# Three input tiles on ScalarE's queue, memory sums and recurrence constant on GpSimd, memory norm spread behind the first value block

## The chip, the cores and the metric

The kernel runs on one core of a Trainium2 chip. The time is that of the device, in microseconds (us), for one execution. The engines are named as the profile names them: PE is TensorE (matrix products), PEld its weight loads, DVE is VectorE, ACT is ScalarE, POOL is GpSimd, SP is SyncE, which only issues DMAs here. Each engine takes its own instructions in a fixed order and waits for the others through semaphores.

## The reference

A two-layer decoder trunk over 1024 positions of width 1024, all in float32. Layer A joins a gated linear recurrence (width 768) with an attention of four heads over 256 memory rows; layer B joins a windowed attention with the same kind of memory attention. Each has an output projection and a SwiGLU feed-forward behind it. What the change touches is the start of layer A:

```python
mem_n = rms_norm(mem, mem_norm)
h = x
for l in range(DEPTH):
    hn = rms_norm(h, norm_mix_pre[l])
    mkv = mem_n @ w_mem_kv[l]
    mk = mkv[..., :MEM_WIDTH].reshape(bsz, n_mem, MEM_HEADS, HEAD_DIM)
    mv = mkv[..., MEM_WIDTH:].reshape(bsz, n_mem, MEM_HEADS, HEAD_DIM)
    if l < N_A_LAYERS:
        proj = hn @ w_in_a[a]
        ...
        y = rg_lru(xr, w_r, b_r, w_i, b_i, lam) * jax.nn.gelu(gate)
    ...
    m_out = memory_attention(mq, mk, mv)
```

In `rg_lru` the decay is `exp(8 * r * log_sigmoid(lam))`. Its `8 * log_sigmoid(lam)` and twice that are the recurrence constant, 6 columns of 128 numbers.

## The kernel before

Activations lie with their 1024 channels on partitions, in 8 tiles of 128, and positions along the row, in two halves of 512. Every matrix product in float32 is made of three: a number is split into a rounded high part (a cast or scaled copy on ScalarE) and a low part (the difference, on VectorE), and TensorE adds low x high, high x high and high x low. So each weight and each activation costs a ScalarE and a VectorE instruction before TensorE can use it. In a tile's name `ah`/`al` are the activation's parts, `wh`/`wl` a weight's, `wraw` the weight as loaded. The names `qs`, `pb`, `ph` are buffers that hold weight parts in the opening (`spare`).

The order on each engine comes from a scheduler that simulates a timeline and is steered by priorities, by `after` (this instruction not before that one) and by `pin`/`place`, which set an instruction among the matmuls collected in `self.mms` at given places.

The opening (`layer_a`, L1033 on) runs like this:

- `inputs(0, ...)` loads the eight tiles of `x` for the first half, one DMA each (L1043, all on SyncE's queue), between pieces of the first two weights (L141). ScalarE makes `ah` (L1048), VectorE `al` (L1049). Then come eight squares on ScalarE (L234, L237), summed on VectorE (L238).
- `rstd` ends a norm: ones-matmuls put the sums into a column (L248), VectorE scales it (L252), GpSimd takes the power -1/2 (L253), and `spread` multiplies it out over 128 partitions on TensorE (L260), from where ScalarE copies it (L264). `rcn` is the first norm's column, `rcm` the memory's. `self.marks` collects these matmuls so that they can be placed.
- `mem_queries` (L447) makes the two memory queries, in the buffers `gt`, with the tiles as they arrive. `lru_in` makes the two products of the first recurrence block (`mm`, L163 to L165).
- `lambda_const` computes the constant by a series, 28 instructions on VectorE of 6 columns each, which may start behind the first norm's column (`prev`, the mean).
- `mem_in` loads the memory in four DMAs (L1061), splits it (L1066, L1067), squares it on ScalarE (L220, L223) and sums it on VectorE (L224).
- `mem_kv` makes the memory's keys (two blocks, L345 to L347, scaled by the spread norm on VectorE, L348) and values (two blocks, L355 to L357, scaled by the column `rcm` on ScalarE, L358). `mem_expand` casts the keys to both halves of the partitions (`mkh`, L321) and takes the low parts (`mkl`, L323).
- The second recurrence block's two products follow, each 24 matmuls, with weights cast at L94 and L95.

Four rules of the code matter. A buffer is given again only when its last reader is done: `gt` has two, `mm` three, `wh` and `wl` two, `wraw` two. The table load on ScalarE stands ahead of the first activation. The instructions of `mem_in` stand behind the first tiles' squares by `after`. And GpSimd had, from the constants at the start to 60 us, only the two powers and the copies of three columns between halves (`halo`, L464).

Of the kernel before, what the change touches and what calls it, by code (L numbers as in the profile page):

```python
# [10 lines left out]
ALU = mybir.AluOpType  # L11
AX = mybir.AxisListType

P = 128
D = 1024
T = 1024
H = 512
KT = D // P
NM = 256
# [24 lines left out]
POST_STEPS = range(4, 20, 2)  # L44
LATE_PRODUCTS, LAST_STEPS = (2, 5, 3), range(36, 132, 12)
OUT_PARTS = {1: (0, 0), 2: (1, 0), 3: (1, 0), 4: (1, 1), 5: (1, 1), 6: (0, 0), 7: (0, 1)}
NO_SYNC = mybir.DependencyInfo(mybir.DependencyClass.NoSync, mybir.DependencyReason.DATA)
SHUF = list(range(8, 16)) + list(range(0, 8)) + list(range(16, 32))


class Trunk:
# [232 lines left out]
        self.mhalf = cp.tile([P, 4], F32, name="mhalf")  # L284
        nc.gpsimd.memset(self.mhalf, -0.5)

    def lambda_const(self, prev):
        nc, cp = self.nc, self.cp
        lam = self.cst[:, C_LAM:C_LAM + NL]
        t = [self.t(f"lam{i}", (P, NL)) for i in range(5)]  # L290
        e, d, s, s2, h = t
        nc.scalar.activation(e, lam, AF.Abs)
        self.table(e, e, AF.Exp, scale=-1.0)
        self.after(nc.vector.tensor_scalar(d, e, 2.0, None, op0=ALU.add), prev)
        nc.vector.reciprocal(d, d)
        nc.vector.tensor_tensor(s, e, d, op=ALU.mult)
        nc.vector.tensor_tensor(s2, s, s, op=ALU.mult)
        self.after(nc.vector.memset(h, 1.0 / 19.0), prev)
# [3 lines left out]
        nc.vector.tensor_tensor(h, h, s, op=ALU.mult)  # L302
        self.after(nc.vector.tensor_scalar(d, lam, 0.0, None, op0=ALU.min), prev)
# [3 lines left out]
        nc.vector.tensor_scalar(self.cl2, self.cl, 16.0, None, op0=ALU.mult)  # L307
        nc.vector.tensor_scalar(self.cl, self.cl, 8.0, None, op0=ALU.mult)

    def kdup_far(self, kf, r, kh, kl, prev):  # L310
        here = slice(r, r + 64)
# [15 lines left out]
        nc.scalar.copy(qs[r:r + 64], qf[r:r + 64])  # L327
        nc.vector.tensor_tensor(qs[64 - r:128 - r], qf[r:r + 64], qs[r:r + 64].bitcast(F32), op=ALU.subtract)

    def mem_kv(self, layer, mact, rcm, rsm):  # L330
        nc = self.nc
        kf, vf = (self.t(t).rearrange("p (i c) -> p i c", i=2) for t in ("gr", "gi"))
        for j in range(2):
            if layer == 0:
                with self.tc.high_priority(offset=WEIGHT_LEAD):
                    w, piece = self.first_weight(self.a["wmk"][layer, j], self.spare(1 - j))
                    for i in range(2):
                        piece(4 * i, 4 * i + 4)
            else:
                whole = self.weight(self.a["wmk"][layer, j])  # L340
                w = [[x[:, 4 * i:4 * i + 4] for x in whole] for i in range(2)]
            ps = self.psum("mm")
            for k in range(KT):
                wh, wl = (x[:, k % 4] for x in w[k // 4])
                nc.tensor.matmul(ps[:, :NM], wh, mact[k][1], start=k == 0, stop=False)  # L345
                nc.tensor.matmul(ps[:, :NM], wh, mact[k][0], start=False, stop=False)
                nc.tensor.matmul(ps[:, :NM], wl, mact[k][0], start=False, stop=k == KT - 1)  # L347
            nc.vector.tensor_tensor(kf[:, j], ps[:, :NM], rsm, op=ALU.mult)  # L348
        wv = [self.weight(self.a["wmv"][layer, :, 4 * j:4 * j + 4], k=4) for j in range(2)]
        for m in range(2):  # L350
            ps = self.psum("mm")
            for k in range(KT):
                wh, wl = wv[k // 4]
                ms = slice(m * P, m * P + P)
                nc.tensor.matmul(ps[:, :NM], mact[k][1][:, ms], wh[:, k % 4], start=k == 0, stop=False)  # L355
                nc.tensor.matmul(ps[:, :NM], mact[k][0][:, ms], wh[:, k % 4], start=False, stop=False)
# [673 lines left out]
    def layer_a(self):  # L1030
        nc, a = self.nc, self.a
# [4 lines left out]
        def inputs(n, before=()):  # L1036
            act, xs, loads = [], [], []
            s = self.t("s")
            for k in range(KT):
                if k in before:  # L1040
                    before[k]()
                x = self.acc_tile()
                loads.append(nc.sync.dma_start(x, a["xT"][k * P:k * P + P, n * H:n * H + H]))  # L1043
# [4 lines left out]
                last = nc.scalar.activation(ah, x, AF.Copy, scale=g)  # L1048
                nc.vector.scalar_tensor_tensor(al, x, g, ah.bitcast(F32), op0=ALU.mult, op1=ALU.subtract)  # L1049
            take = self.sums([(nc.vector, s)], "00000000", ("sq", "sp"))  # L1050
            for k in range(KT):
                ins = take(k, xs[k]) if k == 0 else (take(k, xs[k]), self.square)[1]
                self.after(ins, last)
            return act, self.rstd(s, f"n{n}", "rsn")[1], loads

        def mem_in(square, summed):
            act = []
            s = self.t("s")[:, :NM]
            for q in range(4):
# [21 lines left out]
        mean, prev = self.mean, (self.square, self.summed)  # L1081
        marks = self.marks[:2]
        self.mms = []
        for n in range(2):
# [9 lines left out]
            for j0 in range(0, NL, 2):  # L1094
                cur = []
                for j in (j0, j0 + 1):
# [275 lines left out]
```

## Time and profile before

| | |
|---|---|
| three runs | 1968.11, 1966.99, 1969.09 us; median 1968.11 us |
| the profiled execution | 1966.76 us, its span (first to last instruction) 1964.7 us |
| granted TensorE clock | 0.997 |
| DMA | 361.71 MB, 184 GB/s over the span |
| VectorE, GpSimd busy | 71%, 22% of the span |

Rows of the timeline have the start, the duration, engine, line of the kernel, operation, output and inputs with their shapes, and in brackets how long the engine was idle before and what ended that. A stretch has its length, the busy time of PE, PEld, DVE, ACT and POOL with their counts, the granted clock, the DMA engines' busy share and GB/s. Busy time of TensorE overlaps from one matmul to the next: a matmul of 512 columns lasts 0.39 us and the next one starts 0.23 us behind it.

### The profile page before, as it was taken

Reading aid. Unit: us, or ns where it says so; the run is one execution under the profiler, and the core shown is the slowest. Engines: PE = TensorE matmul, PEld = TensorE weight load, DVE = VectorE, ACT = ScalarE, POOL = GpSimd, SP = SyncE. Lnnn points to the kernel's source line nnn. Section 1 sums busy time; section 2 is a strip of 40 time slices with the busy share of each in tenths; the row PEclk is TensorE's granted clock in tenths of the full one; section 3 lists DMA queues with packets and bytes.
Section 4 is the critical chain, followed back from the end, with each engine's and each line's share of the span. In section 5 each row is a group of like instructions: output and inputs, shape, how many; then the busy total and the mean of one; then the engine's idle time right before and its main releaser. Section 6 shows DMA issues by size and latency. Waiting matters only on the chain.

```text
span 1964.7 us, 27857 instructions
## 1 busy us (share of the span) xinstructions
PE 1935.3 (99%) x9382; PEld 1626.5 (83%) x9382; DVE 1397.8 (71%) x2319; ACT 1015.5 (52%) x1939; POOL 426.0 (22%) x435
## 2 busy tenths in 40 slices
PE   8999999999999999999999999999999999999997
PEld 7887888788888888888788888887888888888887
DVE  8888977976776676455786898669656666754566
ACT  6677974534444444454554778554333333344551
POOL 0122100034443330000035454100223232300001
PEclk9999999999999999999999999999999999999999
DMA  5522536167767789775563333361644544586653
GB/s 186 170 86 81 158 121 228 67 233 250 240 243 276 257 294 319 236 230 176 201 214 141 121 106 108 107 258 43 209 135 166 167 150 157 199 302 195 218 187 129
DMA packets 184686, 361.71 MB, mean 184 GB/s; under 512 B 20448, under 2 KB 26336, under 8 KB 184544
## 3 DMA queue, kind: packets, MB, share of 16 engines
q1 hardware_dynamic: 184544, 359.95, 53.8%
q8 instruction: 73, 1.20, 0.2%
q14 instruction: 69, 0.57, 0.1%
HBM read 251.86 MB, written 105.91 MB: 182 GB/s over the span
## 4 chain that ended last, share of the span: by engine, by line
PE 88%; DVE 6%; ACT 2%; issue 2%; DMA 1%; POOL 1%; SPq 0%; POOLq 0%; DVEq 0%; ACTq 0%
PE mm L699 12%; PE mm L701 12%; PE mm L700 12%; PE mm L807 7%; PE mm L808 7%; PE mm L809 7%; PE mm L165 6%; PE mm L163 6%; PE mm L164 6%; PE oo L1187 1%; PE tt L1180 1%; PE oo L248 1%; PE mm L679 1%; PE mm L678 1%; PE mm L680 1%
## 5 line engine op out<-in xcount | busy, mean ns | idle before, releaser
L94 ACT CAST ch<-wq 128x512 fp32r<-128x512 f32 x311 | 193.4, 622 | 423.6 <-PE mm L700 212.4
L95 DVE TENSOR_TENSOR cl<-wq,ch 128x512 fp32r<-128x512 f32 x311 | 236.2, 760 | 191.8 <-ACT ch L94 118.3
L699 PE MATMUL mm<-al,ch 128*128 128x512 f32 x640 | 249.6, 390 | 2.9 <-ACT c L729 2.9
L700 PE MATMUL mm<-ah,ch 128*128 128x512 f32 x640 | 249.2, 389 | 0.0
L701 PE MATMUL mm<-ah,cl 128*128 128x512 f32 x640 | 249.0, 389 | 0.0
L163 PE MATMUL mm<-al,wh 128*128 128x512 f32 x552 | 218.2, 395 | 0.6 <-ACT wh L94 0.6
L165 PE MATMUL mm<-ah,wl 128*128 128x512 f32 x552 | 216.9, 393 | 0.9 <-DVE wl L95 0.9
L164 PE MATMUL mm<-ah,wh 128*128 128x512 f32 x552 | 216.8, 393 | 0.0
L807 PE MATMUL mm<-tl,ch 128*128 128x512 f32 x532 | 207.4, 390 | 0.6 <-ACT ah L909 0.3
L808 PE MATMUL mm<-th,ch 128*128 128x512 f32 x532 | 207.0, 389 | 0.0
L809 PE MATMUL mm<-th,cl 128*128 128x512 f32 x532 | 206.4, 389 | 0.0
L699 PE MATMUL mm<-tl,ch 128*128 128x512 f32 x480 | 187.4, 390 | 0.2
L701 PE MATMUL mm<-th,cl 128*128 128x512 f32 x480 | 186.5, 389 | 0.4 <-DVE cl L95 0.4
L700 PE MATMUL mm<-th,ch 128*128 128x512 f32 x480 | 186.8, 389 | 0.0
L710 DVE TENSOR_TENSOR c<-c,mm 128x512 f32<-128x512 f32 x120 | 82.3, 686 | 100.7 <-PE mm L701 100.5
L699 PEld LDWEIGHTS mm<-al,ch 128*128 128x128 f32 x640 | 120.2, 188 | 28.4 <-ACT c L729 3.7
L701 PEld LDWEIGHTS mm<-ah,cl 128*128 128x128 f32 x640 | 120.2, 188 | 25.0
L700 PEld LDWEIGHTS mm<-ah,ch 128*128 128x128 f32 x640 | 120.2, 188 | 24.7
L165 PEld LDWEIGHTS mm<-ah,wl 128*128 128x128 f32 x552 | 103.7, 188 | 23.4 <-DVE wl L95 2.1
L719 POOL TENSOR_TENSOR x<-wq,wq 128x512 f32<-128x512 f32 x36 | 52.6, 1461 | 318.7 <-DMA wq<-in_wi_dram 310.8
L163 PEld LDWEIGHTS mm<-al,wh 128*128 128x128 f32 x552 | 103.8, 188 | 21.1 <-ACT wh L94 1.0
L164 PEld LDWEIGHTS mm<-ah,wh 128*128 128x128 f32 x552 | 103.8, 188 | 20.2
(415 smaller groups left out, 4312.4 us busy)
## 6 DMA issues: line engine op xcount, KB each, us to landing
wq<-in_wi_dram SPq DMA_DIRECT2D x168, 256.0 KB, 4.6
xz<-hd SPq DMA_DIRECT2D x154, 256.0 KB, 4.1
th<-xz SPq DMA_DIRECT2D x154, 256.0 KB, 3.5
wp<-in_wf_dram SPq DMA_DIRECT2D x112, 256.0 KB, 4.1
wz<-wp SPq DMA_DIRECT2D x88, 256.0 KB, 2.3
wq<-wz SPq DMA_DIRECT2D x56, 256.0 KB, 3.5
wraw<-in_wa_dram SPq DMA_DIRECT2D x26, 512.0 KB, 3.5
wq<-in_wf_dram SPq DMA_DIRECT2D x42, 256.0 KB, 4.0
```

Source lines behind the costliest of these rows:

```text
L94: self.cast = self.nc.scalar.copy(hi, src)
L95: return (eng or self.nc.vector).tensor_tensor(lo, src, hi.bitcast(F32), op=ALU.subtract)
L163: self.mms += [nc.tensor.matmul(out, wh, al, start=i == 0, stop=False), nc.tensor.matmul(out, wh, ah, start=False, stop=False), nc.tensor. ...
L164: nc.tensor.matmul(out, wh, ah, start=False, stop=False),
L165: nc.tensor.matmul(out, wl, ah, start=False, stop=i == len(ks) - 1)]
L699: ins += [mm(out, wh, xl, start=start and k == 0, stop=False, skip_group_check=not start), mm(out, wh, xh, start=False, stop=False, skip_g ...
L700: mm(out, wh, xh, start=False, stop=False, skip_group_check=not start),
L701: mm(out, wl, xh, start=False, stop=k == 3, skip_group_check=not start)]
L710: add = lambda o, x, y: nc.vector.tensor_tensor(o, x, y, op=ALU.add)
L807: ins += [mm(ps[m], wh[:, m], xl[:, cs], start=start and p == 0, stop=False, skip_group_check=not start), mm(ps[m], wh[:, m], xh[:, cs], s ...
L808: mm(ps[m], wh[:, m], xh[:, cs], start=False, stop=False, skip_group_check=not start),
L809: mm(ps[m], wl[:, m], xh[:, cs], start=False, stop=p == NFB // 2 - 1, skip_group_check=not start)]
```

## The change

Four edits. The first three input tiles of the first half are issued on ScalarE's queue (`HEAD`). `lambda_const` runs on GpSimd but for the reciprocal and the two activations, without its order behind the mean; the fused multiply-add of its end becomes two instructions. The memory's sums run on GpSimd. In the first layer's `mem_kv` the two key blocks are accumulated in `gt` buffers, and the memory norm's spread is ordered behind the last matmul of the first value block.

```diff
+HEAD = 3
...
-    def lambda_const(self, prev):
-        nc, cp = self.nc, self.cp
+    def lambda_const(self):
+        nc, cp, po = self.nc, self.cp, self.nc.gpsimd
...
         self.table(e, e, AF.Exp, scale=-1.0)
-        self.after(nc.vector.tensor_scalar(d, e, 2.0, None, op0=ALU.add), prev)
+        po.tensor_scalar(d, e, 2.0, 0.0, op0=ALU.add, op1=ALU.add)
         nc.vector.reciprocal(d, d)
-        nc.vector.tensor_tensor(s, e, d, op=ALU.mult)
-        nc.vector.tensor_tensor(s2, s, s, op=ALU.mult)
-        self.after(nc.vector.memset(h, 1.0 / 19.0), prev)
+        po.tensor_tensor(s, e, d, op=ALU.mult)
+        po.tensor_tensor(s2, s, s, op=ALU.mult)
+        po.memset(h, 1.0 / 19.0)
         for q in (17, 15, 13, 11, 9, 7, 5, 3, 1):
-            nc.vector.tensor_tensor(h, h, s2, op=ALU.mult)
-            nc.vector.tensor_scalar(h, h, 1.0 / q, None, op0=ALU.add)
...
+            po.tensor_tensor(h, h, s2, op=ALU.mult)
+            po.tensor_scalar(h, h, 1.0 / q, 0.0, op0=ALU.add, op1=ALU.add)
...
-        nc.vector.scalar_tensor_tensor(self.cl, h, -2.0, d, op0=ALU.mult, op1=ALU.add)
...
+        po.tensor_scalar(h, h, -2.0, 0.0, op0=ALU.mult, op1=ALU.add)
+        po.tensor_tensor(self.cl, h, d, op=ALU.add)
...
-    def mem_kv(self, layer, mact, rcm, rsm):
+    def mem_kv(self, layer, mact, rcm, rsm, spread=None):
...
-            ps = self.psum("mm")
+            ps = self.psum("mm" if spread is None else "gt")
...
-                nc.tensor.matmul(ps[:, :NM], mact[k][0][:, ms], wl[:, k % 4], start=False, stop=k == KT - 1)
+                last = nc.tensor.matmul(ps[:, :NM], mact[k][0][:, ms], wl[:, k % 4], start=False, stop=k == KT - 1)
+            if m == 0 and spread is not None:
+                self.after(spread[0], last)
...
-                loads.append(nc.sync.dma_start(x, a["xT"][k * P:k * P + P, n * H:n * H + H]))
+                queue = nc.scalar if n == 0 and k < HEAD else nc.sync
+                loads.append(queue.dma_start(x, a["xT"][k * P:k * P + P, n * H:n * H + H]))
...
-                    self.sumsq(s, mr[:, i], k == 0, NM, ("sp", "sq")[i])
+                    self.sumsq(s, mr[:, i], k == 0, NM, ("sp", "sq")[i], nc.gpsimd)
...
-                        self.lambda_const(mean)
+                        self.lambda_const()
                         mem = mem_in(*prev)
-                        kvf = self.mem_kv(0, *mem)
+                        kvf = self.mem_kv(0, *mem, self.marks[-1])
```

How the order on the engines moves, at three places. First ScalarE at its start; `acc` are the input tiles, `lam` the constant. Before:

```order
L292 ACT_TABLE_LOAD
L292 ACTIVATE lam_65_370<-cst 128x6
L98 ACTIVATE lam_65_370<-lam_65_370 128x6
L94 CAST wh_131<-wraw_130 128x256
L1048 ACTIVATE ah_144<-acc_142,cst 128x512
```

And with the change:

```order
L1048 DMA acc_142<-in_xT_dram 128x512
L1048 DMA acc_154<-in_xT_dram 128x512
L1048 DMA acc_163<-in_xT_dram 128x512
L1053 ACT_TABLE_LOAD
L1053 ACTIVATE ah_144<-acc_142,cst 128x512
L293 ACTIVATE lam_65_370<-cst 128x6
L95 CAST wh_131<-wraw_130 128x256
L1053 ACTIVATE ah_156<-acc_154,cst 128x512
```

Three DMA issues and the table load now stand ahead of the first tile's scaled copy, and the constant's first activation behind it. The table load carries that copy's wait for `cst`.

Second GpSimd around the first norm's power (`rcn`). Before:

```order
L459 MEMSET xr_1021 128x3
L253 TENSOR_TENSOR rcn_45_232<-rcn_45_232,mhalf 128x4
L464 COPY halo_116<-xr_308 128x3
L253 TENSOR_TENSOR rcm_465<-rcm_465,mhalf 128x2
L459 MEMSET xr_1242 128x3
```

With the change, from the end of the constant on:

```order
L308 TENSOR_TENSOR cl<-lam_69_374,lam_66_371 128x6
L309 TENSOR_SCALAR cl_403<-cl 128x6
L310 TENSOR_SCALAR cl<-cl 128x6
L225 TENSOR_TENSOR s_408<-s_408,sq_418 128x256
L254 TENSOR_TENSOR rcn_45_232<-rcn_45_232,mhalf 128x4
L225 TENSOR_TENSOR s_408<-s_408,sp_427 128x256
L225 TENSOR_TENSOR s_408<-s_408,sq_432 128x256
```

The whole constant and the first of the seven memory sums now stand ahead of that power; the other six sums stand between it and the memory's power. On TensorE the spread of `rcn` (L261) now follows the twelfth matmul of the second product at once, and all the memory's key matmuls follow that product; before, fourteen of them stood between.

Third ScalarE and TensorE behind the memory norm's spread. ScalarE before (`gi` is the first value block, `xc` the spread, `gr` the keys):

```order
L358 ACTIVATE gi_474<-mm_561,rcm_465 128x256
L94 CAST mvv_131_689<-gi_474 128x2x64
L94 CAST mvv_134_704<-gi_474 128x2x64
L264 COPY xc_468<-oo_469 128x256
L94 CAST wh_615<-wraw_613 128x1024
L321 CAST mkh_129_687<-gr_473 64x256 x4
L321 CAST mkh_132_702<-gr_473 64x256 x2
L94 CAST wh_621<-wraw_619 128x1024
```

ScalarE with the change:

```order
L362 ACTIVATE gi_475<-mm_562,rcm_466 128x256
L265 COPY xc_469<-oo_470 128x256
L95 CAST mvv_131_690<-gi_475 128x2x64
L95 CAST mvv_134_705<-gi_475 128x2x64
L323 CAST mkh_129_688<-gr_474 64x256 x4
L95 CAST wh_616<-wraw_614 128x1024
L323 CAST mkh_132_703<-gr_474 64x256 x4
L95 CAST wh_622<-wraw_620 128x1024
```

TensorE with the change, a few rows behind the second value block (before, that block is followed by all 24 matmuls of `mm_627`, which is `mm_628` here):

```order
L413 MATMUL ss_1091<-mkl_130_689,qs_1084 128x256
L414 MATMUL ss_1091<-mkh_129_688,qs_1084 128x256
L164 MATMUL mm_628<-al_145,wh_616 128x512
L165 MATMUL mm_628<-ah_144,wh_616 128x512
L164 MATMUL mm_656<-al_145,wh_622 128x512
L165 MATMUL mm_656<-ah_144,wh_622 128x512
L166 MATMUL mm_628<-ah_144,wl_617 128x512
```

Four key casts now stand ahead of the first weight cast and four more ahead of the second; on TensorE two score products of a memory unit (four matmuls, the last two of them shown) and two matmuls with the second weight (`wh_622`) stand ahead of the first one with the first weight's low part (`wl_617`). From the second recurrence block to layer A's output projection the blocks follow one another as before, while scores, gates and transposes fall at other places between their matmuls.

More of the change, by code (lines that the diff above doesn't have):

```diff
@@ L293, in lambda_const @@
         self.table(e, e, AF.Exp, scale=-1.0)
[L294 removed]
+        po.tensor_scalar(d, e, 2.0, 0.0, op0=ALU.add, op1=ALU.add)
         nc.vector.reciprocal(d, d)
[L296 to L298 removed]
+        po.tensor_tensor(s, e, d, op=ALU.mult)
+        po.tensor_tensor(s2, s, s, op=ALU.mult)
+        po.memset(h, 1.0 / 19.0)
         for q in (17, 15, 13, 11, 9, 7, 5, 3, 1):
[L300 to L303 removed]
+            po.tensor_tensor(h, h, s2, op=ALU.mult)
+            po.tensor_scalar(h, h, 1.0 / q, 0.0, op0=ALU.add, op1=ALU.add)
+        po.tensor_tensor(h, h, s, op=ALU.mult)
+        po.tensor_scalar(d, lam, 0.0, 0.0, op0=ALU.min, op1=ALU.add)
         self.cl = cp.tile([P, NL], F32, name="cl")
         self.cl2 = cp.tile([P, NL], F32, name="cl2")
[L306 to L308 removed]
+        po.tensor_scalar(h, h, -2.0, 0.0, op0=ALU.mult, op1=ALU.add)
+        po.tensor_tensor(self.cl, h, d, op=ALU.add)
+        po.tensor_scalar(self.cl2, self.cl, 16.0, 0.0, op0=ALU.mult, op1=ALU.add)
+        po.tensor_scalar(self.cl, self.cl, 8.0, 0.0, op0=ALU.mult, op1=ALU.add)
     def kdup_far(self, kf, r, kh, kl, prev):
@@ L1080, in layer_a @@
                              2: lambda: piece1(2, 4), 4: lambda: piece0(4, 8), 5: lambda: piece1(4, 8)})
-        mean, prev = self.mean, (self.square, self.summed)
+        prev = self.square, self.summed
         marks = self.marks[:2]
```

## The prediction

> **What bounds the kernel now.** I read the page first, then the table of stretches for the first 60 us, then the timeline and the chain of waits there, because every edit lies before the second block of layer A's projections.
>
> ```profile
> span 1964.7 us, 27857 instructions
> PE 1935.3 (99%) x9382; PEld 1626.5 (83%) x9382; DVE 1397.8 (71%) x2319; ACT 1015.5 (52%) x1939; POOL 426.0 (22%) x435
> PE 88%; DVE 6%; ACT 2%; issue 2%; DMA 1%; POOL 1%; SPq 0%; POOLq 0%; DVEq 0%; ACTq 0%
> 0.00:20.00 20.00, 16.70 (x73) 13.21 (x73) 11.84 (x19) 14.18 (x25) 0.91 (x12) 1.00 0.81 272
> 20.00:40.00 20.00, 20.00 (x126) 18.09 (x127) 19.02 (x45) 14.21 (x29) 2.40 (x2) 1.00 0.48 154
> 40.00:60.00 20.00, 18.34 (x102) 15.70 (x101) 16.87 (x46) 11.12 (x24) 0.99 (x3) 1.00 0.31 107
> ```
>
> TensorE is busy 99% of the span and holds 88% of the chain that ended last, so the kernel gains only where TensorE stands idle. (In the stretches the columns after the length are PE, PEld, DVE, ACT, POOL, clock, DMA share, GB/s.) From 0 to 20 us it lacks 3.30 us, from 20 to 40 us nothing, from 40 to 60 us 1.66 us. No edit here can be worth more than about 5 us of 1968, so most of the question is whether it gives back what it takes.
>
> The opening's own end is not TensorE's. These timeline rows (start, duration, engine, line, idle before and its releaser) are its chain:
>
> ```profile
> 4.76 0.72 ACT L1048 ACTIVATE ah<-acc,cst 128x512 fp32r<-128x512 f32 x1 [0.93 <-DMA acc<-in_xT_dram]
> 6.33 0.50 PE L447 MATMUL gt<-al,wh 128*128 128x512 f32 x1 [0.65 <-DVE al L1049]
> 11.92 0.72 ACT L1048 ACTIVATE ah<-acc,cst 128x512 fp32r<-128x512 f32 x1 [0.96 <-DMA acc<-in_xT_dram]
> 17.59 1.04 ACT L94 CAST wh<-wraw 128x1024 fp32r<-128x1024 f32 x1
> 18.66 1.23 DVE L95 TENSOR_TENSOR wl<-wraw,wh 128x1024 fp32r<-128x1024 f32 x1
> 19.94 0.50 PE L165 MATMUL mm<-ah,wl 128*128 128x512 f32 x1 [0.25 <-DVE wl L95]
> 2.00:4.00 2.00, 2.00 (x11) 2.00 (x11) 0.13 (x1) 0.83 (x4) 0.00 (x0) 1.00 0.75 247
> 4.00:8.00 4.00, 3.34 (x18) 2.54 (x17) 2.02 (x5) 2.39 (x5) 0.00 (x0) 1.00 0.93 254
> ```
>
> The fifth input tile lands at 11.9; from there ScalarE works without a pause to the cast at 17.59, VectorE makes the low half, and TensorE goes on at 19.94. So it is the fifth tile that counts, not the first three. The last two rows are stretches: from 4 to 8 us the DMA engines are 0.93 busy, in the two microseconds before only 0.75, so 0.5 us of their time there is unused.
>
> **Three tiles on ScalarE's queue.** No DMA by ScalarE is in this trace; the nearest row is SyncE's issue of the first tile.
>
> ```profile
> 0.72 1.28 ACT L292 ACT_TABLE_LOAD   x1 [0.72 <-PEq L1361]
> 1.63 0.42 SPq L1043 DMA_DIRECT2D acc<-in_xT_dram  x1
> 2.64 0.21 ACT L292 ACTIVATE lam<-cst 128x6 f32<-128x6 f32 x1 [0.63 <-DMA cst<-in_cst_dram]
> ```
>
> Three issues of 0.42 us take ScalarE from 0.72 to 2.0, when it otherwise loads its table. The load now stands behind them and takes over the wait for cst (landing at 2.6), so it runs to 3.9, still ahead of the 4.76 at which the first tile was worked on. The first tile leaves 0.9 us earlier (0.72 against 1.63), and the first matmul may start some 0.7 us before 6.33. But the fifth tile lies behind the same 2.1 MB in both orders (five tiles of 256 KB, weight pieces of 768 KB, cst of 70 KB), and only the 0.5 us that the engines lacked between 2 and 4 us can be won. Bounds 0 and 0.5 us; I take **-0.3 us** at 19.94, the middle.
>
> The Trainium skill, "DMA: Bandwidth & Descriptors", section "Issuing engines are not separate DMA queues", says that queues of several engines feed the same 16 DMA engines and that only issue time is saved, which is "usually small relative to the DMA itself". With queues of their own the three tiles would bring their 0.9 us through to the fifth tile and the sum would be 0.6 lower; by that rule they don't, and the shares above agree with it.
>
> **Recurrence constant on GpSimd.** 27 small operations move. What leaves VectorE is worth nothing by itself, since most of it stood between 20 and 40 us, where TensorE misses nothing. Of them 26 follow the reciprocal, which VectorE reaches at about 7.8 us by my estimate (it stands behind the second tile's low half and a weight piece, 1.5 us after the first matmul's 6.33). What one costs on GpSimd is bounded by two rows of the same 3-column copy:
>
> ```profile
> 33.99 1.22 DVE L95 TENSOR_TENSOR wl<-wraw,wh 128x1024 fp32r<-128x1024 f32 x1
> 34.07 1.19 POOL L464 COPY halo<-xr 128x3 f32<-128x3 f32 x1 [5.10 <-DVE xr L462]
> 35.12 0.42 DVE L224 TENSOR_TENSOR s<-s,sq 128x256 f32<-128x256 f32 x1
> 54.61 0.19 POOL L464 COPY halo<-xr 128x3 f32<-128x3 f32 x1 [5.62 <-DVE xr L462]
> 8.00:13.00 5.00, 4.02 (x16) 3.04 (x17) 3.21 (x6) 3.02 (x6) 0.00 (x0) 1.00 0.99 330
> ```
>
> Alone it takes 0.19 us; started while VectorE reads two SBUF tensors it ends with that operation, after 1.19. So the chain ends between 12.7 and 38.7 us. In the new order VectorE has 28 operations of that kind from the reciprocal to the first norm's column, and it idles 1.8 of the 5 us from 8 to 13 (the last row); one GpSimd operation per VectorE operation, and half a dozen in the gaps, puts the end near 25. That is the value I take, and it costs nothing, because the next GpSimd instruction (the first memory sum) has no data before 27.0. VectorE's next operation after the blocked copy took its usual 0.42 us, so I charge VectorE nothing.
>
> **Memory sums on GpSimd.** Seven 128x256 additions (0.42 us each on VectorE) move. GpSimd's nearest row is 128x512 in 1.46 us, so half, 0.7 us, and up to a VectorE operation more when blocked. What matters is the place: the first of them now stands ahead of the power that ends the first norm.
>
> ```profile
> 26.57 0.42 ACT L223 ACTIVATE sq<-a 128x256 f32<-128x256 f32 x1
> 26.85 0.69 DVE L95 TENSOR_TENSOR pb<-wraw,pb 128x512 fp32r<-128x512 f32 x1
> 27.76 1.21 POOL L253 TENSOR_TENSOR rcn<-rcn,mhalf 128x4 f32<-128x4 f32 x1 [26.29 <-DVE lam L298]
> L719 POOL TENSOR_TENSOR x<-wq,wq 128x512 f32<-128x512 f32 x36 | 52.6, 1461 | 318.7 <-DMA wq<-in_wi_dram 310.8 <-DMA wp<-in_wf_dram 7.9
> 28.74 0.28 PE L345 MATMUL mm<-al,pb 128*128 128x256 f32 x1
> 30.41 1.05 PE L260 MATMUL oo<-ident,rcn 128*128 128x128 f32 x8
> ```
>
> The addition gets its square at 27.0, finds VectorE's low half running until 27.5, ends near 28.2, and the power, 1.21 us as before, near 29.4. Before, it was done at 28.97 and TensorE asked at 30.41, after fourteen memory matmuls that stood ahead of the spread, 0.12 us each from the first one's start at 28.74. In the new order they stand behind it, so TensorE asks at 28.74. The slack of 1.44 us becomes a wait of 29.4 - 28.74: **+0.7 us** (bounds: 0, and 1.9 if addition and power each lose to one more VectorE operation of 0.6). The other six additions must be done when TensorE reaches the ones-matmuls, near 36.6: seven at 1.19 from 27.5 make 35.8. No charge, but no slack either.
>
> **Memory norm spread behind the first value block.** What goes is the second row here, 1.03 us; what follows is the interesting part.
>
> ```profile
> 41.00 0.50 PE L248 MATMUL oo<-ones,s 128*128 128x1 f32 x4
> 42.54 0.71 PE L260 MATMUL oo<-ident,rcm 128*128 128x128 f32 x4 [1.03 <-POOL rcm L253]
> 43.43 0.36 ACT L264 COPY xc<-oo 128x256 f32<-128x256 f32 x1
> 44.53 0.42 DVE L348 TENSOR_TENSOR gr<-mm,xc 128x256 f32<-128x256 f32 x1
> 44.66 1.05 ACT L94 CAST wh<-wraw 128x1024 fp32r<-128x1024 f32 x1 [0.86 <-PE mm L356]
> 45.61 2.52 ACT L321 CAST mkh<-gr 64x256 fp32r<-64x256 f32 x6
> 46.01 1.22 DVE L95 TENSOR_TENSOR wl<-wraw,wh 128x1024 fp32r<-128x1024 f32 x1
> 46.25 0.40 PE L164 MATMUL mm<-ah,wh 128*128 128x512 f32 x1
> 47.28 0.50 PE L165 MATMUL mm<-ah,wl 128*128 128x512 f32 x1 [0.63 <-DVE wl L95]
> 48.16 1.05 ACT L94 CAST wh<-wraw 128x1024 fp32r<-128x1024 f32 x1
> ```
>
> Count from the spread's start, A (42.54 before). Before, TensorE would have issued the third matmul of the next block at A+3.94 (0.23 us after 46.25) and did at A+4.74: 0.80 us lost to the low half. In the new order ScalarE makes four key casts ahead of the first weight cast and four more ahead of the second, and TensorE's queue has four score matmuls and then two matmuls with that second weight, ahead of the third matmul of the first. ScalarE: the copy of the spread ends at about A+1.1, the first key block at A+1.6, four casts of 0.42 give A+3.3, a weight cast 0.95 gives A+4.25, four casts A+5.9, the second weight cast A+7.0. TensorE: from A to the second matmul it took 3.71 us; with four score matmuls of 0.12 ahead and one place of 0.23 further on it asks for the second weight at A+4.4. It waits 2.6 us, against 0.80. Sum of this part: -1.03 - 0.80 + 2.6 = **+0.8 us** (bounds: -1.8, if the casts fall elsewhere, and +1.6).
>
> **The sum.** -0.3 + 0 + 0.7 + 0.8 = +1.2 us on the profiled execution's 1966.76 us (span 1964.7 and 2.06 around it), that is 1967.96. The median of the three runs shown is 1968.11, 1.35 above that execution, so I put the forecast at 1968.11 + 1.2 = 1969.3. Behind 60 us the blocks keep their order, but score, gate and transposed products fall at other places up to the first layer's output projection. There TensorE waits three times (the waits up to 400 us: total, times, longest):
>
> ```profile
> PE gt L491 <- ACT gr L98: 2.1, 2, 1.3
> PE mm L163 <- ACT wh L94: 0.6, 1, 0.6
> ```
>
> They make 2.7 us; I take no change, with plus or minus 2.7 us as bounds.
>
> **Rivals.** *Gain as the words of the change have it:* the 1.03 us goes, the casts come in time, so that the 0.80 stays as it is, the power is not late, and the opening gives 0.3: -1.3 us, 1966.8. For it: ScalarE is busy 11.12 of the 20 us from 40 to 60. Against: the order of the casts.
>
> *GpSimd's queue runs over (the slower side):* the 26 constant operations stand ahead of the power. They decide from 0.74 us each, (27.0-7.8)/26; past that each microsecond of their end is one of TensorE's at the first spread. At 0.9 us they end at 31.2, 4.2 us later: +5.4 us in all, 1973.5. For it: 1.19 us for the blocked copy. Against: the gaps from 8 to 13 us.
>
> *GpSimd blocks VectorE in the opening:* from 11.9 to 18.7 us about 12 of the small operations fall; if each holds VectorE up for its 0.19 us, the low half at 18.66 is 2.3 us later, +3.5 us, 1971.6. Against it stands the 0.42 us at 35.12. The Trainium skill, "SBUF — State Buffer", section "Who interferes with whom", calls the shared port pair an exclusive lock that the first comer holds for the whole instruction, which would make this the rule. The blocked copy agrees with it in one direction; the other direction is not in the rows shown.
>
> *The tiles land no earlier* (the change doesn't do what it says): the -0.3 falls away, 1969.6. *The interleaving behind 60 us* takes away the three waits (1966.6) or doubles them (1972.0).
>
> **How the numbers follow.** Forecast 0.45 (its own range 1967.3 to 1971.3), gain 0.25, queue overrun 0.12, blocked VectorE 0.06, no earlier tiles 0.05, interleaving 0.04 and 0.03. The range reaches from 1966.0, under the gain's 1966.8 by the spread of the runs, to 1972.1, and leaves out the overrun and the tail of the gain. 0.2% is 3.9 us, about what a measurement of this kernel can tell from no change: faster means under 1964.2, which takes the gain and the lost waits together, 0.03; slower means over 1972.05, nearly all of the overrun and a part of the two below it, 0.12; the same 0.85.
>
> **What would show it.** Right: the fifth tile's cast starts 0.2 to 0.5 us before 11.92; the constant's last operation on GpSimd ends before 27; a wait of about 0.7 us on TensorE ahead of the first spread, none ahead of the memory spread, and about 2.6 us between the score matmuls and the second weight's first. Wrong: a wait of several us at the first spread (overrun), a wait at the ones-matmuls of the memory sum (the additions are slower than 1.2 us), or the third matmul going on within 0.8 us (the casts are not what counts).

## The result, and the profile after

The changed kernel takes 1977.62 us (median of 6 runs, 1976.56 to 1980.36) against 1967.45 us for the kernel before in the same session: ratio 1.0056, 95% interval 1.0045 to 1.0067. It is 10 us slower, outside the range given. The profiled execution took 1978.88 us, with a span of 1976.7.

The page of the changed kernel first, then its stretches (length, then PE, PEld, DVE, ACT, POOL, granted clock, DMA share, GB/s):

```profile
span 1976.7 us, 27864 instructions
PE 1941.2 (98%) x9382; PEld 1629.9 (82%) x9382; DVE 1392.7 (70%) x2285; ACT 1015.0 (51%) x1939; POOL 444.2 (22%) x470
PE 86%; DVE 5%; ACT 4%; issue 2%; DMA 1%; POOL 1%; SPq 0%; POOLq 0%; DVEq 0%; ACTq 0%
44.00:50.00 6.00, 3.79 (x24) 2.97 (x23) 5.83 (x13) 5.63 (x12) 0.00 (x0) 1.00 0.06 13
50.00:54.00 4.00, 4.00 (x12) 3.14 (x11) 3.75 (x8) 1.53 (x5) 0.10 (x1) 0.57 0.30 117
260.00:270.00 10.00, 9.19 (x43) 7.25 (x42) 6.21 (x10) 9.93 (x16) 0.61 (x1) 1.00 0.15 52
270.00:282.00 12.00, 6.29 (x24) 4.25 (x23) 8.54 (x12) 10.28 (x16) 0.61 (x1) 0.88 0.34 111
282.00:286.00 4.00, 4.00 (x11) 3.12 (x10) 1.98 (x4) 1.67 (x3) 0.00 (x0) 0.51 0.19 65
```

The page shows little: one point of TensorE's share, 2 points of the chain. The stretches show two places where TensorE idles and then runs at half clock. From 50 to 54 us it is "busy" all the time, but at a clock of 0.57 it starts 12 products where the kernel before starts 21. The same two places in the kernel before:

```profile
44.00:50.00 6.00, 5.37 (x33) 4.44 (x32) 5.90 (x14) 5.17 (x10) 0.10 (x1) 1.00 0.24 83
50.00:54.00 4.00, 4.00 (x21) 3.40 (x20) 3.90 (x10) 2.62 (x6) 0.00 (x0) 1.00 0.25 79
270.00:282.00 12.00, 12.00 (x63) 10.22 (x62) 7.52 (x12) 6.87 (x13) 0.17 (x1) 1.00 0.31 96
282.00:286.00 4.00, 4.00 (x23) 3.44 (x22) 0.47 (x1) 0.75 (x2) 0.85 (x1) 1.00 0.37 131
```

Busy time hides a low clock, so I compare by a **lag** that I work out from the timeline: a product's start minus the undisturbed length of all TensorE work ahead of it (0.227 us for 512 columns, 0.12 for 256, 0.07 for 128). The lag at 60 us is 11.1 us before and 13.9 after; at 300 us it is 20.9 and 31.8. So 2.8 us are lost in the opening and 8.1 us between 60 and 300 us. Of the 2.8 two come back up to 260 us; from 260 to 300 us, at the end of layer A, where nothing was edited, ten go. Three openings of the same program (before, late_gate, late_score below) have lags of 11.1, 11.9 and 11.3 at 60 us; less than 1 us is not read.

What TensorE waits for at 274 us (timeline: start, duration, engine, line, and in brackets the idle time before and who ended it):

```profile
274.55 0.50 PE L164 MATMUL mm<-al,ph 128*128 128x512 f32 x1 [0.91 <-ACT ph L95]
276.14 0.50 PE L433 MATMUL oo<-pl,mvv 128*128 128x512 f32 x1 [0.86 <-DVE pl L96]
280.82 0.80 PE L166 MATMUL mm<-ah,ph 128*128 128x512 f32 x1 [3.94 <-DVE ph L96]
281.42 0.63 PE L164 MATMUL mm<-al,ph 128*128 128x512 f32 x1
281.85 0.63 PE L165 MATMUL mm<-ah,ph 128*128 128x512 f32 x1
```

The two `ph` buffers serve twice there: for the high parts of the transposed probabilities of layer A's last memory unit, and for the high and the low part of the last half of the last output weight, which is split once that unit is through. (`pl` holds the low parts of the probabilities alone.) 0.91, 0.86 and 3.94 us make the 5.71 us that TensorE lacks from 270 to 282. Behind them products start every 0.43 us, not every 0.23.

The chain behind the 3.94, by the timelines of TensorE, ScalarE and VectorE; after:

```profile
247.17 0.28 PE L413 MATMUL ss<-mkl,qs 128*128 128x256 f32 x1
266.64 0.60 PE L428 MATMUL tt<-ident,pb 128*128 128x128 f32 x4
266.79 1.28 ACT L99 ACT_TABLE_LOAD   x1
270.96 1.28 ACT L99 ACT_TABLE_LOAD   x1
273.40 0.58 ACT L95 CAST ph<-tt 128x512 fp32r<-128x512 f32 x1
273.88 0.62 ACT L95 CAST ph<-wraw 128x512 fp32r<-128x512 f32 x1
277.70 1.28 DVE L520 TENSOR_TENSOR_SCAN a<-gr,carry,gi 128x512 f32<-128x512 f32 x1
280.08 0.69 DVE L96 TENSOR_TENSOR ph<-wraw,ph 128x512 fp32r<-128x512 f32 x1
```

And before:

```profile
238.36 0.28 PE L409 MATMUL ss<-mkl,qs 128*128 128x256 f32 x1
256.55 0.60 PE L424 MATMUL tt<-ident,pb 128*128 128x128 f32 x4
261.75 0.58 ACT L94 CAST ph<-tt 128x512 fp32r<-128x512 f32 x1
265.94 0.62 ACT L94 CAST ph<-wraw 128x512 fp32r<-128x512 f32 x1
269.77 1.28 DVE L516 TENSOR_TENSOR_SCAN a<-gr,carry,gi 128x512 f32<-128x512 f32 x1
270.96 0.67 DVE L95 TENSOR_TENSOR ph<-wraw,ph 128x512 fp32r<-128x512 f32 x1
272.45 0.39 PE L165 MATMUL mm<-ah,ph 128*128 128x512 f32 x1
```

The last unit's scores come 8.8 us later than before, its last transposes 10.1, the low half 9.1, while TensorE's own lag at 260 us is only 0.8 us more than before. TensorE had taken projection products from behind the late scores, and then had none left. On ScalarE the cast of the last probabilities (`ph<-tt`) now stands behind both table loads of the last recurrence pair; before, it stood between them. On VectorE the low half stands behind that pair's second scan in both kernels. Before, TensorE used that low half at 272.45 without a wait (the last row); it was there at 271.63. The slack was under 1 us.

### The profile page after: what moved, and what is told of

It reads as the page before. It is cut to its first block, busy times and chain, and to the rows that moved or that the text cites. A ratio compares the mean times of both kernels' runs of the same rounds, so it can differ in the third digit from the quotient of the medians.

```text
span 1976.7 us, 27864 instructions
## 1 busy us (share of the span) xinstructions
PE 1941.2 (98%) x9382; PEld 1629.9 (82%) x9382; DVE 1392.7 (70%) x2285; ACT 1015.0 (51%) x1939; POOL 444.2 (22%) x470
## 4 chain that ended last, share of the span: by engine, by line
PE 86%; DVE 5%; ACT 4%; issue 2%; DMA 1%; POOL 1%; SPq 0%; POOLq 0%; DVEq 0%; ACTq 0%
PE mm L703 12%; PE mm L705 12%; PE mm L704 12%; PE mm L811 7%; PE mm L812 7%; PE mm L813 7%; PE mm L164 6%; PE mm L166 6%; PE mm L165 6%; PE oo L1192 1%; PE tt L1185 1%; PE mm L683 1%; PE oo L249 1%; PE mm L682 1%; PE mm L684 1%
```

## The experiments

By program order on TensorE, the second half of the last unit's scores stands at row 1101 before and 1136 after; the last two pairs of gate products start at 1156/1159 before and 1196/1200 after. "Growth" is the lag at 300 us minus that at 60.

| run | scores, gates (row) | median us | ratio to before (95%) | lag at 60 | growth |
|---|---|---|---|---|---|
| before | 1101, 1156 | 1966.9 to 1967.5 | 1 | 11.1 | 9.8 |
| changed | 1136, 1196 | 1977.62 | 1.0056 (1.0045 to 1.0067) | 13.9 | 17.9 |
| h_alone | 1101, 1156 | 1966.22 | 0.9992 (0.9983 to 1.0001) | 10.4 | 9.8 |
| l_alone | 1099, 1146 | 1968.65 | 1.0005 (0.9996 to 1.0014) | 11.9 | 9.8 |
| s_alone | 1136, 1196 | 1983.46 | 1.0079 (1.0066 to 1.0092) | 19.2 | 17.4 |
| g_alone | 1136, 1196 | 1973.67 | 1.0032 (1.0020 to 1.0044) | 9.1 | 16.6 |
| late_gate | 1101, 1194 | 1967.40 | 1.0004 (0.9995 to 1.0013) | 11.9 | 10.4 |
| after_hold | 1112, 1168 | 1971.60 | 1.0023 (1.0014 to 1.0033) | 13.1 | 12.3 |
| hg_hold | 1109, 1163 | 1969.53 | 1.0013 (1.0004 to 1.0022) | 8.6 | 13.3 |
| no_sums | 1136, 1196 | 1976.29 | 1.0048 (1.0034 to 1.0062) | 11.4 | 16.7 |
| late_score | 1134, 1196 | 1976.07 | 1.0045 (1.0033 to 1.0058) | 11.3 | 17.5 |
| after_tail | 1136, 1196 | 1972.63 | 1.0022 (1.0013 to 1.0031) | 13.9 | 11.2 |
| hg_tail | 1136, 1196 | 1966.61 | 0.9999 (0.9990 to 1.0008) | 8.6 | 10.8 |
| l_gap | 1099, 1146 | 1966.36 | 0.9996 (0.9987 to 1.0005) | 10.8 | 9.0 |
| after_cast | 1136, 1196 | 1967.95 | 1.0004 (0.9995 to 1.0013) | 10.8 | 12.3 |
| all_but_sums | 1136, 1196 | 1967.02 | 1.0004 (0.9995 to 1.0013) | 8.7 | 12.3 |

**One edit at a time.** Each takes the lines of one edit from the diff above into the kernel before: h_alone the input tiles, l_alone the constant, s_alone the sums, g_alone the norm.

```diff
# h_alone
...
+                queue = nc.scalar if n == 0 and k < HEAD else nc.sync
# l_alone
+        nc, cp, po = self.nc, self.cp, self.nc.gpsimd
...
# s_alone
+                    self.sumsq(s, mr[:, i], k == 0, NM, ("sp", "sq")[i], nc.gpsimd)
# g_alone
...
+            ps = self.psum("mm" if spread is None else "gt")
...
+                self.after(spread[0], last)
...
```

> The kernel before with only the three input tiles issued by ScalarE's queue. In program order the rows of the engines behind the opening stand as before, the last two gate products of layer A at rows 1156 and 1159. Theory ORDER (the loss is the later place of the last score and gate products of layer A): no loss here, 0 to -0.4 us, TensorE's idle time from 240 to 300 us as before (about 2 us). Theory OPENING (the loss comes from the opening, the later landing of the constants at 4.4 us): +1 us or more. Theory NORM (the memory norm's place): 0.

> The kernel before with only the recurrence constant on GpSimd. The last gate products stand at rows 1146 and 1157, earlier than before. Theory ORDER: within 2 us of before, rather faster, no stretch of half clock near 280 us. Theory SHARING (GpSimd's small operations slow VectorE, or the constant comes late): +1 to +4 us, and the loss lies ahead of 60 us.

> The kernel before with only the seven memory sums on GpSimd. The last gate products stand at rows 1196 and 1200, as in the changed kernel, though nothing of layer A was edited. Theory ORDER: slower by 5 to 10 us, with TensorE idle 4 to 7 us in all between 265 and 285 us and a stretch of half clock behind it. Theories NORM and OPENING: within 1 us of before.

> The kernel before with only the memory norm's spread behind the first value block, the key products in the gates' PSUM tiles. The last gate products stand at rows 1196 and 1199. Theory ORDER: slower by 5 to 10 us with the idle time at 265 to 285 us. Theory NORM (the key casts ahead of the second weight cast): the loss lies at 44 to 56 us alone, 2 to 4 us, and nothing near 280 us.

The tiles and the constant, which leave the scores about where they were, are within 0.1% of before, and their growth is 9.8 us as before. The sums alone and the norm alone each bring the late order, and a growth of 17.4 and 16.6. The norm's edit does in the opening what its words say: at 60 us it is 2 us ahead of before, and all of that and more goes near 275 us. The prices don't add up (about -1, +1, +16 and +6 against +10 together), as a term for each edit would have to.

s_alone lost more than expected, because it also loses 8 us in the opening. There ScalarE waits for GpSimd to free the buffers of its squares. The copy of the first norm's spread, which VectorE's `xr` needs, now stands behind two squares more and behind a weight's cast that waits for its load until 32.74; it starts at 33.70, against 31.50 before. VectorE then has operations of the constant and a weight's low half ahead of `xr`, which starts at 37.84, against 33.32. The last row is TensorE, 2.42 us late, and from 38 to 44 us its granted clock is 0.50:

```profile
29.62 0.42 ACT L223 ACTIVATE sp<-xc 128x256 f32<-128x256 f32 x1 [0.72 <-POOL s L224]
30.77 0.42 ACT L223 ACTIVATE sq<-xc 128x256 f32<-128x256 f32 x1 [0.73 <-POOL s L224]
33.70 0.58 ACT L264 COPY rsn<-oo 128x512 f32<-128x512 f32 x1
38.57 0.58 PE L345 MATMUL mm<-al,qs 128*128 128x256 f32 x1 [2.42 <-DVE xr L462]
```

**Which part of the late order.** late_gate sets one number in the kernel before, and moves the gates alone; late_score moves the scores by one constraint in the kernel before.

```diff
# late_gate
-GATE_PLACE, WARM, MEM_LATE, UNITS_A = 80, 11, 2, ((0, 1, 0), (2, 0, 0))
+GATE_PLACE, WARM, MEM_LATE, UNITS_A = 122, 11, 2, ((0, 1, 0), (2, 0, 0))
# late_score, in mem_unit and in mix_out
+                self.score = ins if b == 2 else self.score
...
+            self.after(self.score, self.mms[74])
```

> The kernel before with one number changed, the place among the output projection's products from which the last two gate products of layer A may stand, 80 to 122: on TensorE they move from rows 1156 and 1159 to 1194 and 1197, about where the changed kernel has them, and no other row of TensorE changes its order there; the opening is that of before. Theory ORDER (gate place alone): slower by 5 to 10 us, idle time near 270 to 285 us and half clock behind it. Rival CHAIN (the gates are only the last member; what counts is that the whole chain of score, exponentials and gates is late): 1 to 4 us, since the scores keep their place. Rival OPENING (all is made in the opening): 0.

> The kernel before with one constraint more: the second half of the last unit's scores may stand only behind the 75th product of the output projection. TensorE's scores go from row 1101 to 1134, and from there the scheduler gives the very order of the run with the norm's edit alone (gates at 1196 and 1199, two products of the sixth tile, then the seventh); the opening is that of before. Theory CHAIN (late scores put the last unit's transposes, and with them the split of the last output weight, behind the last recurrence pair in the queues of ScalarE and VectorE): 1972 to 1977 us, with the three waits 0.9, 0.9 and 3.9 us of the changed kernel (for ph from ScalarE, pl and ph from VectorE) near 275 us and half clock behind them. Rival STOCK (the loss needs a TensorE that was ahead): 1967 to 1969 us.

My first theory fell with late_gate: gates 38 rows later cost nothing that the runs can tell. There the last weight is split ahead of the late gates' recurrence: its low half starts at 265.67, though the last pair's gates come at 261.34 and not at 250.96. The scores do it: with the opening of before and one constraint the kernel loses 9 us. TensorE's waits in late_score from 260 to 300 us (engine, line, for whom; total, times, longest), all of them:

```profile
PE mm L166 <- DVE ph L96: 3.9, 1, 3.9
PE mm L164 <- ACT ph L95: 1.4, 1, 1.4
PE oo L431 <- DVE pl L96: 0.9, 1, 0.9
```

These are the changed kernel's three. So neither GpSimd nor ScalarE's queue nor a TensorE that ran ahead is needed for the loss of 60 to 300 us; late scores are enough.

**Holding the order, and leaving out the sums.** after_hold is the changed kernel, hg_hold the kernel before with the tiles and the norm's edit; both keep 48 products of the output projection, from place 50 on (counted from 0), behind the last unit's scores. no_sums is the changed kernel with the sums on VectorE.

```diff
# after_hold and hg_hold, in mix_out; lastscore is the last unit's last score product
...
             self.after(self.gate, self.mms[GATE_PLACE])
+            self.place(self.mms, [[self.lastscore]], [50])
# no_sums
-                    self.sumsq(s, mr[:, i], k == 0, NM, ("sp", "sq")[i], nc.gpsimd)
+                    self.sumsq(s, mr[:, i], k == 0, NM, ("sp", "sq")[i])
```

> The changed kernel with one constraint more: the output projection's products from the 50th on stand behind the last unit's scores. TensorE's last scores go from row 1136 to 1112, the last gates from 1196 and 1200 to 1168 and 1171, near before's; the opening is that of the changed kernel. Theory ORDER: the loss at 260 to 300 us goes (about 8 us), the one at 40 to 60 us stays (about 2.8 us): 1969 to 1972 us. If the loss near 280 us has another cause: 1976 to 1979 us.

> The kernel before with the three tiles on ScalarE's queue, the memory norm's spread behind the first value block, and the same constraint; no sums and no constant on GpSimd. The last scores go from row 1136 to 1109, the gates from 1196 and 1199 to 1163 and 1166. Theory ORDER: the run with the norm's edit alone stood 2.0 us ahead of before at 60 us and lost about 10 us between 265 and 285; with the order held that gain and the tiles' 0.7 us stay: 1963 to 1966 us, faster than before. If the constraint only moves the wait: 1969 to 1973 us.

> The changed kernel with the memory sums back on VectorE; the late order stays (last scores at row 1136, gates at 1196 and 1199). Theory SUMS (the sums on GpSimd cost the opening: ScalarE's squares wait for their buffers, and the norm's copy stands behind them): the lag at 60 us is 3 to 5 us less than in the changed kernel, the loss at 265 to 285 us stays: 1971 to 1975 us. If the sums cost nothing there: 1976 to 1979 us.

The constraint takes 6 of the 10 us away in after_hold. In hg_hold the gain of the opening doesn't last, against my expectation: TensorE then waits in front of the scores themselves, 2.3 us for ScalarE's `pb` at 240 us (in after_hold 3.2 us for VectorE's `xl` at 242, in front of a gate). An order forced on TensorE doesn't make ScalarE or VectorE earlier. no_sums missed as well. It gained 2.5 us at 60 and not the 3 to 5 expected, because a new wait of 2.9 us stood at the first norm's power; l_gap, below, looks at that.

**The queues at the end.** after_tail and hg_tail leave TensorE's late order and change two queues: the last recurrence pair's first exponential (`self.decay`) stands behind the cast of the last half of the last weight, its first product (`self.step`) behind the low part of that half.

```diff
...
+                self.final = self.cast, low
...
+            self.after(self.decay, self.final[0])
+            self.after(self.step, self.final[1])
```

> The changed kernel with two constraints more and the late order of TensorE left alone: on ScalarE the last pair's first exponential stands behind the cast of the last output weight, on VectorE the last pair's first product behind the low half of that weight. Theory CHAIN with the queues as its last step: the waits for ph and pl near 275 us go, and the half clock with them: 1968 to 1971 us. If a late recurrence itself is what TensorE waits for: 1975 to 1980 us.

> The kernel before with the three tiles on ScalarE's queue, the norm's spread behind the first value block, and the two constraints of the queues; sums and constant on VectorE. Theory CHAIN: the norm's edit alone was 2.0 us ahead of before at 60 us and lost it all near 275 us; without that loss 1963 to 1966 us, faster than before. If ScalarE's and VectorE's work in layer A is the bound: 1967 to 1970 us.

With two constraints on queues the three waits shrink to one of 0.6 us, and the half clock goes (the same stretch as above, in after_tail):

```profile
270.00:282.00 12.00, 11.40 (x51) 9.12 (x50) 6.91 (x10) 11.65 (x18) 1.23 (x2) 1.00 0.15 51
```

The growth falls from 17.9 to 11.2 us, the time to 1972.63, a little over what I expected: a wait of 1.1 us for a square now precedes the norm at 284 us, and the 2.8 us of the opening stay. (Only one execution of a run has a trace, and a stretch of half clock in it need not be in the others: the eleven of after_tail lie between 1967.42 and 1974.93 us.) hg_tail has the opening's 2.5 us at 60 us, but no time that differs from before.

**The opening.** l_gap adds three small, unused operations on VectorE to l_alone. after_cast adds to after_tail that ScalarE's key casts stand behind the second projection weight's cast. all_but_sums is the changed kernel with the sums on VectorE, l_gap's operations and after_tail's constraints.

```diff
# l_gap
...
+        self.after(nc.vector.tensor_scalar(gap[0], lam, 2.0, None, op0=ALU.add), mean)
+        self.after(nc.vector.memset(gap[1], 1.0), mean)
+        nc.vector.reciprocal(gap[0], gap[0])
# after_cast; weighed is the second projection weight's cast
...
-            nc.scalar.copy(kh[o:o + 64], kf[r:r + 64])
+            ins = nc.scalar.copy(kh[o:o + 64], kf[r:r + 64])
+            if self.weighed is not None:
+                self.after(ins, self.weighed)
```

> The run with the constant alone, and three small operations of 128x6 on VectorE (one scalar operation, one fill, one reciprocal, results unused) where the kernel before has three of the constant. In the run without them GpSimd's power for the first norm took 4.02 us against 1.21 us before. Theory STREAK (GpSimd's operation waits through VectorE's unbroken run of two-input operations, and small operations of one input let it in): 1.2 to 1.5 us for the power, the spread of the first norm 2.5 to 3 us earlier, 1965.5 to 1968 us. Rival (the power is slow because GpSimd just ran the constant, or for its length alone): 3.5 to 4.1 us, time as in the run with the constant alone.

> The changed kernel with the two constraints of the queues at the end of layer A and one more in the opening: on ScalarE the eight key casts stand behind the cast of the second projection weight. Theory CAST (the changed kernel's loss at 44 to 56 us is the key casts ahead of that weight: 1.9 us of waiting, and some 1.8 us because TensorE then runs four microseconds at half clock): the lag at 60 us falls from 13.9 by 3 to 4 us, no half clock near 50 us: 1967 to 1970 us. If the sums on GpSimd cost the opening in another place: 1971 to 1974 us.

> The changed kernel without the memory sums on GpSimd (VectorE adds them), with three small operations on VectorE in its run of subtractions, and the two constraints of the queues at the end of layer A. Theories STREAK and CHAIN together: the wait for the first norm's power (2.9 us in the run without the sums) falls under 0.6 us, the three waits near 275 us fall to 1.5 us at most: 1964 to 1967 us. If moving the constant to GpSimd costs more than that: 1968 to 1972 us.

In l_alone (first five rows) VectorE runs one operation of two SBUF inputs after another behind the first norm's mean, and GpSimd's power takes 4.02 us; in l_gap (last three) the small ones stand between, and it takes 1.29:

```profile
27.10 4.02 POOL L253 TENSOR_TENSOR rcn<-rcn,mhalf 128x4 f32<-128x4 f32 x1 [11.56 <-DVE rcn L252]
27.33 0.68 DVE L95 TENSOR_TENSOR ph<-wraw,ph 128x512 fp32r<-128x512 f32 x1
27.93 0.41 DVE L224 TENSOR_TENSOR s<-s,sq 128x256 f32<-128x256 f32 x1
28.27 0.68 DVE L95 TENSOR_TENSOR qs<-wraw,qs 128x512 fp32r<-128x512 f32 x1
29.21 0.68 DVE L95 TENSOR_TENSOR pb<-wraw,pb 128x512 fp32r<-128x512 f32 x1
27.27 0.17 DVE L295 TENSOR_SCALAR gap<-cst 128x6 f32<-128x6 f32 x1
27.38 0.06 DVE L296 MEMSET gap<- 128x6 f32 x1
27.44 1.29 POOL L253 TENSOR_TENSOR rcn<-rcn,mhalf 128x4 f32<-128x4 f32 x1 [11.39 <-DVE gap L296]
```

So the constant's operations on VectorE, which looked like pure load, were what let GpSimd in. The power is settled; what it is worth in time isn't. The lag at 60 us falls by 1.1 us from l_alone to l_gap and the time by 2.3, but neither run can be told from the kernel before, and a few rows near the spread changed order as well.

after_cast's lag at 60 us falls by 3.0 us to before's, and its stretch from 50 to 54 has the full clock again; with both repairs the changed kernel is level with before. all_but_sums is level too: the constant on GpSimd costs nothing that the runs can tell once the power isn't held up. No version beats the kernel before by more than the runs can tell. hg_tail and all_but_sums pass 60 us 2.5 and 2.4 us ahead, and give 1.0 and 2.5 us back by 300. In both TensorE waits 1.3 us for the last weight's low half near 269 us and 1.1 us for the norm's square near 279, where the kernel before has waits of 0.6 and 0.8 us (at 174 and 251); that is the 1.0. all_but_sums runs at half clock behind the second wait as well (0.68 and 0.50 in the stretches from 280 and 282 us), hg_tail at 1.00.

## Why the prediction was wrong, step by step

The opening's chain in the changed kernel (timeline):

```profile
4.45 1.28 ACT L1053 ACT_TABLE_LOAD   x1 [4.45 <-DMA cst<-in_cst_dram]
7.40 0.47 PE L451 MATMUL gt<-al,wh 128*128 128x512 f32 x1 [1.09 <-DVE al L1054]
10.91 0.73 ACT L1053 ACTIVATE ah<-acc,cst 128x512 fp32r<-128x512 f32 x1 [0.67 <-DMA acc<-in_xT_dram]
19.71 0.50 PE L166 MATMUL mm<-ah,wl 128*128 128x512 f32 x1 [0.31 <-DVE wl L96]
24.47 0.31 POOL L310 TENSOR_SCALAR cl<-cl 128x6 f32<-128x6 f32 x1
29.15 1.05 PE L261 MATMUL oo<-ident,rcn 128*128 128x128 f32 x7 [0.48 <-POOL rcn L254]
34.75 0.74 POOL L225 TENSOR_TENSOR s<-s,sq 128x256 f32<-128x256 f32 x1
45.21 1.05 ACT L95 CAST wh<-wraw 128x1024 fp32r<-128x1024 f32 x1
46.16 1.66 ACT L323 CAST mkh<-gr 64x256 fp32r<-64x256 f32 x4
47.85 1.05 ACT L95 CAST wh<-wraw 128x1024 fp32r<-128x1024 f32 x1
48.94 0.50 PE L164 MATMUL mm<-al,wh 128*128 128x512 f32 x1 [1.91 <-ACT wh L95]
```

- **Tiles, -0.3 us at 19.94: within what can be read.** 19.71, 0.23 earlier. Only the end was right: the constants land behind the three tiles, so the table load waits to 4.45 and the first product starts 1.07 us later, not 0.7 earlier. The fifth tile came 1.0 earlier, not 0.2 to 0.5. The unchanged opening of late_gate reached this product at 20.78, so the runs' spread is larger than the term.
- **Constant, end near 25, no cost: right here, for a reason I hadn't seen.** It ended at 24.78. But in l_alone and no_sums its leaving VectorE made the power 4.0 us; in the changed kernel the first sum goes ahead and the power takes 1.23. (That it is this sum which keeps the power short was not tried by itself.)
- **Sums, +0.7 at the spread: 0.48; done by 35.49 against 35.8.** Right as waits, but incomplete. The step said nothing of the other end: it takes the sums on GpSimd beside the norm's edit to put the key casts ahead of the second weight (in g_alone and no_sums, where VectorE adds, they stand behind it).
- **Norm's spread, +0.8: right mechanism, too small.** Forecast were 2.6 us of waiting for the second weight; 1.91 came, and 0.30 ahead of the scores, against 1.03 and 0.63 before. What I left out is the clock: 4 us at 0.57 lose another 1.7 us. The wait and the clock together make some 2.2 us in place of the 0.8, which is most of the step from 1.2 us to 2.8 at 60. after_cast, which moves these casts alone, takes 3.0 of it back.
- **The later interleaving, "I take no change, with plus or minus 2.7 us as bounds": the step that failed.** It measured 8.1 us in place of nothing: 5.7 of new waiting and, by my estimate, some 2.6 from half clock (1.2 us of products up to 282, 4 us up to 286). The three waits that the bounds were made of went from 2.7 to 2.2 us. I had seen that scores, gates and transposes fall at other places, and bounded what that may cost by the waits that the kernel before has there. A new order makes waits that the old one hasn't, and the old trace does show how near they are, by the slack of what is used next. Here that was under 1 us for the last weight's low half, behind a chain that the new order made 9 us later.

Of the rivals, the queue overrun came nearest in time (1973.5) and was not what happened. GpSimd does block VectorE, unlike my reading of one row (the 128x256 subtraction `gwl` at 29 to 30 us takes 0.94 us in the changed kernel and 0.95 in s_alone, not 0.42), but in the changed kernel no wait of TensorE follows from it there.

Not settled: why the scheduler's own timeline puts the scores 35 rows later with either the sums or the norm's edit, and not with the constant. Only its results were compared.

## What to carry to other kernels

Where a scheduler orders the work, an edit in one stage is an edit in every later stage: compare the new order up to the point where it agrees with the old again, and price the rows that moved by the slack that the old trace shows for their last users, not by the waits it shows. Follow a moved product through the in-order queues of the other engines, since the one that pays here was a weight split queued behind a recurrence. And an engine relieved of small operations may lose the gaps that another lived on.

## What the runs showed of the hardware

**A wait under 2 us can cost as much again in clock.** In the changed kernel TensorE's longest gap near 48 us is 1.91 us, and from 50.5 to 53.5 its products start 0.43 us apart, at a granted clock of 0.60 and 0.55 in the two stretches of 2 us. The Trainium skill, "TensorE: Matmul & The Clock Gate", section "HAM oscillation — how this bites in real kernels", has the rule that there should be no idle gaps over about 3.4 us. The half rate agrees with that page, the gap doesn't: TensorE was busy for 1.04 of the 2 us up to 48 and 1.06 of the next 2. Gaps of 1.03 and 0.63 us in the same place (before) left the clock at 1.00. But the size of the gap doesn't decide alone: in no_sums TensorE stands idle for 2.92 us, up to 30.88, and the clock stays at 1.00, and of the two kernels with the same waits near 269 and 279 us, hg_tail and all_but_sums, only one went to half clock. What decides is not shown here.

**GpSimd waits through a whole run of VectorE operations.** The first norm's power on 128x4 takes 4.02 and 4.03 us in l_alone and no_sums, the two runs with VectorE's run unbroken and no sum ahead of the power, and 1.02 to 1.30 us in the fourteen others. The Trainium skill, "SBUF — State Buffer", section "Who interferes with whom", says that a VectorE instruction with two SBUF inputs contends with a GpSimd instruction that reads SBUF; the runs agree, and show more than one instruction's wait.
